# Building the routing weights of two quarters beside all up-projection units of the second quarter

## The chip, the cores and the metric

The kernel runs on one core of one Trainium2 chip. The metric is the device time of one execution in microseconds (us); less is better. The kernel before takes 2519.42 us, the median of three runs (2518.37 to 2523.47).

The core's engines each take their own instructions strictly in the order in which the program lists them, and they meet only at semaphores: PE (TensorE, matrix products), DVE (VectorE), ACT (ScalarE), POOL (GpSimd), and SP, whose queue issues most of the loads.

## The reference

One decoder layer for 256 tokens of width 2048. The first sub-layer (convolution and attention) isn't touched by the change. The second is a retrieval of single-neuron experts: 16384 experts, an expert being a pair (e1, e2) of 128 x 128, of which each token picks 16 for each of 8 heads.

```
idx = e1 * PEER_NKEYS + e2
g = jax.nn.softmax(top, axis=-1)
def chunk(args):
    xc, ic, gc = args
    u = jnp.take(w_up, ic, axis=0)
    a = jax.nn.gelu(jnp.einsum('td,tkd->tk', xc, u), approximate=False)
    return jnp.einsum('tk,tkd->td', gc * a, jnp.take(w_down, ic, axis=0))
```

Inputs and outputs are float32.

## The kernel before

The kernel computes the retrieval densely. For each of the 128 rows e1 it forms the activation gelu(x . w_up) of 128 experts (e2) for all 256 tokens, multiplies it by a routing weight that is zero where the token didn't pick the expert, and multiplies the product by w_down. Rows go in four quarters q of EQ = 32 rows. Two buffers CB[0] and CB[1], each of 128 x (32 rows x 256 tokens), hold the weighted activations of an even and an odd quarter.

**Units and halves.** Work comes as units of one 1 MB load and two halves each. `Stream.run` (line 214) writes out the order by hand: for half s it first emits "a" of half s+3, then "b" of half s+2, then whatever came due (what was appended to `after` of half s-1, in that order), then the matmuls of half s. All engines' instructions are listed in that order.

- An up half (`up_unit`, line 1233) of n = 0 or 1: "a" transposes half of a weight row on DVE (L1250, tile `wt`, 2 buffers) and casts it on ACT to the high part `hi` (L84, 4 buffers). "b" subtracts, `lo` = `wt` - `hi` (L88, 3 buffers), on POOL or on DVE, as the argument `pool_lo` says. Its 24 matmuls (L1265 to L1267) are three products of high and low parts. After every second row `up_done` (line 1285) takes two rows from PSUM through gelu on ACT.
- A down half (`down_unit`, line 1392): ACT casts weights and activations to high parts (`hi` L84, `cch` L1413), DVE subtracts both low parts (L88, `ccl` L1418), PE does 12 matmuls of 512 columns (L1435 to L1438). A quarter's down work goes in two passes, d = 0 and 1, one for each half of the output columns.
- A gate step (`gate_c`, line 1318; called by `gate_step`, line 1372) makes the routing weights of a pair of quarters for a block of NT = 8 tokens. `build` makes one-hot tiles on DVE: `oh2` (L1331), `oh1` (L1334), and three `ohg` (L1338), all bf16 from SBUF. `product` multiplies them on PE (L1347, 24 matmuls) into PSUM tile `gps`. `apply` multiplies CB[0] by the weights of the even quarter on DVE (L1354), and puts the weights of the odd quarter into CB[1] by an ACT copy (L1359). Step b does apply(b-2), build(b), product(b-1), so 32 blocks need 34 steps.

**The order around the change.** First the 32 up units of quarter 0 run, with every `lo` on POOL, and beside them the top-k selection on DVE. Then 18 up units of quarter 1 run alone ("solo"), every `lo` on POOL, with one gate step after each half. Their activations can't go into CB[1], where the weights are being put, so gelu writes them to a side tile `H` of 16 rows (L1298), and DVE multiplies them into CB[1] later (`weigh`, L1304). Then the remaining 14 up units of quarter 1, every `lo` on DVE, are interleaved with the 16 down units of quarter 0, d = 0; then come the 16 down units of d = 1; and so on. The second pair of quarters has its gate steps in quarter 1's d = 1 pass. Between units of the four interleaved parts `add_units(..., 0.25)` puts one unit of the modulation weights (L344 to L347: a 1 MB load, four ACT operations, POOL additions) after every fourth unit, 16 in all, until the list is empty.

Of the kernel before, what the change touches and what calls it, by code (L numbers as in the profile page):

```python
# [8 lines left out]
F32 = mybir.dt.float32  # L9
# [4 lines left out]
AF = mybir.ActivationFunctionType  # L14
OP = mybir.AluOpType
# [3 lines left out]
P = 128  # L19
T = 256  # L20
# [13 lines left out]
EQ = 32  # L34
# [32 lines left out]
def layer_kernel(ctx, tc, x, c, norm1_g, norm2_g, w_ada, b_ada, w_in, conv_dw, conv_db, conv_ln_g,  # L67
                 conv_ln_b, w_conv_out, b_conv_out, q_norm_g, k_norm_g, w_attn_o, w_out, peer_w_q,
                 peer_sub_keys, peer_w_up, peer_w_down, out):
    nc = tc.nc  # L70
# [6 lines left out]
    main = ctx.enter_context(tc.tile_pool(name="main", bufs=1))  # L77
# [4 lines left out]
    def split_a(h, src):  # L82
        h.hi = main.tile([P, 1024], F32R, name="hi", tag="hi", bufs=HI_BUFS)
        nc.scalar.copy(h.hi, src)  # L84
# [154 lines left out]
    st = Stream()  # L239
    T2 = {}  # L240
# [26 lines left out]
    big16 = main.tile([P, 2, D], F32, name="xin", tag="big16")  # L267
# [455 lines left out]
    def add_units(us, ada_rate=0.0):  # L723
        for u in us:
            st.add(u)
            ada_turn[0] += ada_rate
            while ada_turn[0] >= 1.0 and ada_list:
                ada_turn[0] -= 1.0
                st.add(ada_list.pop())
# [500 lines left out]
    C = {}  # L1230
    CB = []
# [42 lines left out]

    NT = 8
    late = []

    def c_row(q, r, n=1):  # L1280
        if q < 3:
            return CB[q % 2][:, r * T:(r + n) * T]
        return CB[1].rearrange("p (b e t) -> p e b t", e=EQ, t=NT)[:, r:r + n]

    def up_done(q, r, ps):

        if q % 2 == 0:
            nc.scalar.activation(c_row(q, r, 2), ps.rearrange("p r t -> p (r t)"), AF.Gelu)
            return
        if q == 1:  # L1290
            if r == 0:
                C["H"] = main.tile([P, 16, T], F32, name="H", tag="big16")
            h = C["H"][:, r % 16:r % 16 + 2].rearrange("p r t -> p (r t)")

            weigh(r - 14)
        else:
            h = T2["pool"].tile([P, 768], F32, name="hrow", tag="ohg", bufs=2)[:, 0:512]
        nc.scalar.activation(h, ps.rearrange("p r t -> p (r t)"), AF.Gelu)  # L1298
        if q == 3:
            h = h.rearrange("p (r b t) -> p r b t", r=2, t=NT)  # L1300

        def times():
            c = c_row(q, r, 2)
            nc.vector.tensor_tensor(c, c, h, op=OP.mult)  # L1304
        late.append((r, times))
        if q == 3:
            st.at(1, lambda: weigh(r + 2))

    def weigh(upto):
        while late and late[0][0] < upto:  # L1310
            late.pop(0)[1]()

    def weigh_some():
        while late:
            weigh(late[0][0] + 2)
            yield 0.6, 0

# [1 line left out]
    def gate_c(p):  # L1321
        nb = T // NT
        state = {}

        def build(b):

            pairs = lambda v: v.rearrange("p (b t) -> p b t", t=2)
            ts = slice(b * NT, (b + 1) * NT)
            nb2, ne = NT // 2, 2 * EQ
            o2 = T2["pool"].tile([P, nb2, P, 2], BF, name="oh2", tag="oh2", bufs=2)  # L1330
            nc.vector.tensor_tensor(o2, T2["iota"][:, None].to_broadcast([P, nb2, P, 2]),  # L1331
                                    pairs(T2["e2T"][:, ts])[:, :, None].to_broadcast([P, nb2, P, 2]), op=OP.is_equal)
            o1 = T2["pool"].tile([P, nb2, ne, 2], BF, name="oh1", tag="oh1", bufs=1)
            nc.vector.tensor_tensor(o1, T2["iota"][:, None, p * ne:(p + 1) * ne].to_broadcast([P, nb2, ne, 2]),  # L1334
                                    pairs(T2["e1T"][:, ts])[:, :, None].to_broadcast([P, nb2, ne, 2]), op=OP.is_equal)
            og = T2["pool"].tile([P, 3, nb2, ne, 2], BF, name="ohg", tag="ohg", bufs=2)
            for i in range(3):
                nc.vector.tensor_tensor(og[:, i], o1, pairs(T2["gp"][:, i, ts])[:, :, None].to_broadcast([P, nb2, ne, 2]),  # L1338
                                        op=OP.mult)
            state["o", b] = o2, og  # L1340

        def product(b):
            o2, og = state.pop(("o", b))
            ps = T2["ps"].tile([P, NT, 2 * EQ], F32, name="gps", tag="m", bufs=2)
            for t in range(NT):
                for i in range(3):
                    nc.tensor.matmul(ps[:, t, :], lhsT=o2[:, t // 2, :, t % 2], rhs=og[:, i, t // 2, :, t % 2],  # L1347
                                     start=i == 0, stop=i == 2)
            state["p", b] = ps.rearrange("p t e -> p e t")

        def apply(b):
            ps = state.pop(("p", b))
            cv = CB[0].rearrange("p (e t) -> p e t", e=EQ)[:, :, b * NT:(b + 1) * NT]
            nc.vector.tensor_tensor(cv, ps[:, 0:EQ], cv, op=OP.mult)  # L1354
            if p == 0:
                cv = CB[1].rearrange("p (e t) -> p e t", e=EQ)[:, :, b * NT:(b + 1) * NT]
            else:
                cv = CB[1][:, b * T:(b + 1) * T].rearrange("p (e t) -> p e t", e=EQ)
            nc.scalar.copy(cv, ps[:, EQ:2 * EQ])  # L1359

        for b in range(nb + 2):
            if 0 <= b - 2 < nb:
                apply(b - 2)
            if b < nb:
                build(b)
            if 0 <= b - 1 < nb:
                product(b - 1)
            yield
# [3 lines left out]
    def gate_step(p):  # L1372
        next(gates[p], None)

    def finish_gate(p):
        for _ in gates[p]:
            pass
# [9 lines left out]
    def down_unit(q, d, r, whole=False):  # L1387


        u = Unit(None, [])  # L1390
# [8 lines left out]
        for n in range(2):  # L1399
            rr = r + n  # L1400
            h = Half(mm=None)

            def a(h, rr=rr, n=n):
                if rr == 0 and d == 0:
                    if q % 2 == 0:
                        finish_gate(q // 2)
                    else:
                        weigh(EQ)
                split_a(h, u.raw[:, n * 1024:(n + 1) * 1024])

# [58 lines left out]

    def y_done(q, d, ps, t, c):  # L1470
        if q == 0 and d == 0 and t == 0 and c == 0:
            weigh(EQ)
            Y["acc"] = main.tile([P, 2, D], F32, name="y", tag="big16")
        cs = slice(d * 1024 + c * 512, d * 1024 + (c + 1) * 512)
        y = Y["acc"][:, t, cs]
        if q == 0 and c == 0:
            nc.scalar.copy(y, ps[t][c])
        elif q == 0:
            nc.vector.tensor_copy(y, ps[t][c])
        elif q < 3:  # L1480
            nc.vector.tensor_tensor(y, ps[t][c], y, op=OP.add)
        else:
            fin = T2["pool"].tile([P, 1024], F32, name="fin", tag="wt", bufs=2)[:, 0:512]
            nc.vector.tensor_tensor(fin, ps[t][c], Y["g2"][:, cs], op=OP.mult)
            nc.vector.tensor_tensor(fin, fin, y, op=OP.add)
            nc.sync.dma_start(out[0, t * P:(t + 1) * P, cs], fin)
# [26 lines left out]
    busy = lambda r, n: True  # L1513
    none = lambda r, n: False
    some = lambda r, n: n == 1 and r % 2 == 1
    add_units([up_unit(0, r, busy) for r in range(EQ)])
    mark_up1 = len(st.halves)
    nsolo = 18
    solo = [up_unit(1, r, busy) for r in range(nsolo)]
    for u in solo:  # L1520
        for h in u.halves:
            h.after.append(lambda: gate_step(0))
    solo[-1].halves[-1].after.append(lambda: st.spread(weigh_some()))
    add_units(solo)
    marks = []
    first_down = (0.5, 0, 1, 0)
    ada_turn[0] = 0.0
    ada_list[:] = [u for ch in range(4) for u in ada_rest(5 * D + ch * 512, gate_done(1, ch), late=True)][::-1]
    for q in range(4):
        if q < 3:  # L1530
            ups = [up_unit(q + 1, r, some if q == 2 else none) for r in range(nsolo if q == 0 else 0, EQ)]
        else:
            ups = []
        downs = [down_unit(q, 0, r) for r in range(0, EQ, 2)]
        nu, nd = len(ups), len(downs)
        seq = sorted([((i + 0.5) / nu, 0, i) for i in range(nu)] + [((i + first_down[q]) / nd, 1, i) for i in range(nd)])
        for _, kind, i in seq:
            add_units([downs[i] if kind else ups[i]], 0.25)
        assert q < 1 or not ada_list
        m1 = len(st.halves)  # L1540
        downs = [down_unit(q, 1, r, q == 1 and r % 4 == 2) for r in range(0, EQ, 2)]
        if q == 1:
            for u in downs:
                for h in u.halves:
                    h.after.append(lambda: gate_step(1))
            for h in st.halves[-2:]:
                h.after.append(lambda: gate_step(1))
        add_units(downs)
        marks.append((m1, len(st.halves)))
# [66 lines left out]
```

## Time and profile before

| | us |
|---|---|
| median of three runs | 2519.42 |
| the profiled execution | 2518.21 |
| its span, first to last instruction | 2516.4 |
| PE busy in it | 2426.6 (96%) |
| DVE busy | 1854.2 (74%) |
| ACT busy | 1120.8 (45%) |
| POOL busy | 530.3 (21%) |

The profile is of one execution. A busy PE counts matmuls that overlap each other, so its share is an upper mark; where PE has gaps, they are real. DVE's durations contain any time in which an instruction had started and could not proceed. The times of a stretch are counted from the span's start.

### The profile page before, as it was taken

The page shows a single profiled execution, that of the slowest core. Times are in us where ns is not written, and L with a number is a line of the kernel's source. Part 1 is how long each engine was busy: PE and PEld are TensorE (multiplying, and loading weights), DVE is VectorE, ACT ScalarE, POOL GpSimd, SP SyncE. Part 2 cuts the span into 40 slices and gives each one's busy share as a digit, 9 for nine tenths or more (in the row PEclk, how much of TensorE's full clock was granted, in tenths as well). Part 3 has the DMA queues.
Part 4 walks back from the last instruction along what each step waited for, and adds up shares of the span by engine and source line. Part 5 has one row for each costly group of instructions (what it writes and reads, how often), then busy time and mean ns, then how long its engine had stood idle before and what let it go on. Part 6 is the DMA issues. An engine that isn't in the chain of part 4 may idle for free.

```text
span 2516.4 us, 39750 instructions
## 1 busy us (share of the span) xinstructions
PE 2426.6 (96%) x15728; PEld 2056.6 (82%) x15728; DVE 1854.2 (74%) x2642; ACT 1120.8 (45%) x1477; POOL 530.3 (21%) x262
## 2 busy tenths in 40 slices
PE   7999889999999899988999999999999999999998
PEld 4667677777766799988889988999987899988877
DVE  2655679886454569897998787877799777667776
ACT  5333345444334444443335555555443344445454
POOL 1000000000000007786552234332000111124023
PEclk9999999999999999999999999999999999999999
DMA  9887346777899978777557866899844777766563
GB/s 329 297 301 251 117 136 210 257 251 267 279 298 294 204 159 178 158 167 152 110 124 220 234 218 194 222 226 238 204 156 135 185 181 185 188 186 214 194 209 117
DMA packets 261178, 518.73 MB, mean 206 GB/s; under 512 B 16400, under 2 KB 57568, under 8 KB 260352
## 3 DMA queue, kind: packets, MB, share of 16 engines
q1 hardware_dynamic: 258912, 507.61, 70.4%
q0 software_dynamic: 2048, 8.58, 1.0%
q8 instruction: 123, 2.02, 0.4%
q14 instruction: 63, 0.52, 0.1%
q10 hardware_dynamic: 32, 0.01, 0.0%
HBM read 511.94 MB, written 4.19 MB: 205 GB/s over the span
## 4 chain that ended last, share of the span: by engine, by line
PE 71%; DVE 10%; POOL 3%; issue 2%; DMA 1%; ACT 1%; SPq 0%; DVEq 0%; POOLq 0%; ACTq 0%
PE aps L1267 6%; PE aps L1265 6%; PE aps L1266 6%; PE y L1435 6%; PE y L1436 6%; PE y L1438 5%; PE z L429 5%; PE z L431 4%; PE z L430 4%; PE z L1436 3%; PE z L1438 3%; PE z L1435 3%; POOL lo L88 3%; DVE wt L1250 2%; PE ada L330 2%
## 5 line engine op out<-in xcount | busy, mean ns | idle before, releaser
L88 DVE TENSOR_TENSOR lo<-raw,hi 128x1024 fp32r<-128x1024 f32 x456 | 561.8, 1237 | 376.3 <-issue 112.6
L84 ACT CAST hi<-raw 128x1024 fp32r<-128x1024 f32 x504 | 526.6, 1051 | 520.6 <-PE zv L559 103.1
L1267 PE MATMUL aps<-h2hi,lo 128*128 128x256 f32 x2048 | 582.0, 284 | 8.6 <-POOL lo L88 8.5
L1265 PE MATMUL aps<-h2hi,hi 128*128 128x256 f32 x2048 | 584.3, 285 | 0.4 <-ACT hi L84 0.4
L1266 PE MATMUL aps<-h2lo,hi 128*128 128x256 f32 x2048 | 580.7, 284 | 0.0
L84 ACT CAST hi<-wt 128x1024 fp32r<-128x1024 f32 x256 | 269.3, 1052 | 470.7 <-DVE wt L1250 427.6
L88 POOL TENSOR_TENSOR lo<-wt,hi 128x1024 fp32r<-128x1024 f32 x116 | 292.7, 2529 | 611.1 <-PE aps L1267 497.1
L1267 PEld LDWEIGHTS aps<-h2hi,lo 128*128 128x128 f32 x2048 | 394.0, 192 | 11.2 <-POOL lo L88 11.2
L1265 PEld LDWEIGHTS aps<-h2hi,hi 128*128 128x128 f32 x2048 | 394.1, 192 | 2.6 <-ACT hi L84 0.6
L1266 PEld LDWEIGHTS aps<-h2lo,hi 128*128 128x128 f32 x2048 | 394.3, 193 | 2.0 <-issue 0.2
L1250 DVE STREAM_TRANSPOSE wt<-raw 128x1024 f32<-128x1024 f32 x256 | 315.8, 1237 | 28.2 <-POOL lo L88 23.7
L1418 DVE TENSOR_TENSOR ccl<-C,cch 128x256 fp32r<-128x256 f32 x248 | 198.9, 803 | 96.7 <-PE z L1438 57.6
L1435 PE MATMUL y<-hi,cch 128*128 128x512 f32 x608 | 241.1, 397 | 0.0
L1436 PE MATMUL y<-lo,cch 128*128 128x512 f32 x608 | 237.3, 390 | 0.0
L88 DVE TENSOR_TENSOR lo<-wt,hi 128x1024 fp32r<-128x1024 f32 x140 | 171.8, 1229 | 27.3 <-PE aps L1267 14.0
L1438 PE MATMUL y<-hi,ccl 128*128 128x512 f32 x608 | 187.6, 390 | 0.0
L88 POOL TENSOR_TENSOR lo<-raw,hi 128x1024 fp32r<-128x1024 f32 x48 | 117.0, 2436 | 245.9 <-PE z L1436 123.6
L347 POOL TENSOR_TENSOR acc<-acc,raw 128x512 f32<-128x512 f32 x60 | 101.4, 1689 | 261.0 <-ACT raw L346 240.3
L1413 ACT CAST cch<-C 128x256 fp32r<-128x256 f32 x248 | 99.8, 403 | 123.6 <-PE z L1436 101.9
L1436 PE MATMUL z<-lo,cch 128*128 128x512 f32 x384 | 149.5, 389 | 2.2 <-DVE lo L88 2.2
L1435 PE MATMUL z<-hi,cch 128*128 128x512 f32 x384 | 149.5, 389 | 1.0 <-ACT cch L1413 1.0
L1438 PEld LDWEIGHTS y<-hi,ccl 128*128 128x128 f32 x608 | 114.2, 188 | 24.4
(295 smaller groups left out, 3965.7 us busy)
## 6 DMA issues: line engine op xcount, KB each, us to landing
raw<-in_peer_w_up_dram SPq DMA_DIRECT2D x512, 256.0 KB, 6.0
raw<-in_peer_w_down_dram SPq DMA_DIRECT2D x128, 1024.0 KB, 5.1
raw<-in_w_ada_dram SPq DMA_DIRECT2D x86, 1024.0 KB, 7.1
raw<-in_w_in_dram SPq DMA_DIRECT2D x73, 1024.0 KB, 5.3
raw<-in_w_out_dram SPq DMA_DIRECT2D x64, 256.0 KB, 5.2
raw<-in_peer_w_q_dram SPq DMA_DIRECT2D x64, 256.0 KB, 7.1
raw<-in_w_in_dram SPq DMA_DIRECT2D x22, 512.0 KB, 8.9
raw<-in_w_ada_dram SPq DMA_DIRECT2D x20, 512.0 KB, 5.2
```

Source lines behind the costliest of these rows:

```text
L84: nc.scalar.copy(h.hi, src)
L88: eng.tensor_tensor(h.lo, src, h.hi.bitcast(F32), op=OP.subtract)
L347: nc.gpsimd.tensor_tensor(acc, acc, src, op=OP.add)
L429: nc.tensor.matmul(z, lhsT=ah, rhs=hi[:, kk], start=first, stop=False)
L1250: nc.vector.transpose(wt.rearrange("p j g a -> p g j a"), u.raw.rearrange("p (g j a) -> p g j a", g=4, a=32)[:, :, n * 8:(n + 1) * 8, :])
L1265: nc.tensor.matmul(z, lhsT=hi[:, jj], rhs=qh["hi"][:, j, :], start=j == 0, stop=False)
L1266: nc.tensor.matmul(z, lhsT=hi[:, jj], rhs=qh["lo"][:, j, :], start=False, stop=False)
L1267: nc.tensor.matmul(z, lhsT=lo[:, jj], rhs=qh["hi"][:, j, :], start=False, stop=j == NK - 1)
L1418: nc.vector.tensor_tensor(cl, row, ch, op=OP.subtract)
L1435: nc.tensor.matmul(z, lhsT=ch, rhs=hi, start=first, stop=False)
L1436: nc.tensor.matmul(z, lhsT=ch, rhs=lo, start=False, stop=False)
L1438: nc.tensor.matmul(z, lhsT=cl, rhs=hi, start=False, stop=last)
```

## The change

All 32 up units of quarter 1 run alone before any down unit; each unit's first half has its `lo` on DVE, the second on POOL. The 34 gate steps are spread over the first 62 of these 64 halves. Rows and blocks of tokens now meet in either order. `have["t"]` counts the tokens whose weights are in CB[1], `have["rows"]` the rows whose activations are there. When two rows are finished, `up_done` puts gelu straight into CB[1] for tokens without weights, and for those with weights into `H`, which DVE multiplies into CB[1] at once. When a block of weights is finished, `apply` multiplies by it the rows that are there (a second DVE operation from PSUM), and copies it for the other rows. The deferred `weigh` of quarter 1 and `weigh_some` go. Quarter 0's d = 0 part then has down units only.

```diff
@@ up_done
         if q == 1:
-            if r == 0:
-                C["H"] = main.tile([P, 16, T], F32, name="H", tag="big16")
-            h = C["H"][:, r % 16:r % 16 + 2].rearrange("p r t -> p (r t)")
-            weigh(r - 14)
-        else:
-            h = T2["pool"].tile([P, 768], F32, name="hrow", tag="ohg", bufs=2)[:, 0:512]
+            c = c_row(q, r, 2).rearrange("p (r t) -> p r t", r=2)
+            t0 = have["t"]
+            if t0 < T:
+                nc.scalar.activation(c[:, :, t0:], ps[:, :, t0:], AF.Gelu)
+            if t0 > 0:
+                if "H" not in C:
+                    C["H"] = main.tile([P, 16, T], F32, name="H", tag="big16")
+                h = C["H"][:, r % 16:r % 16 + 2, 0:t0]
+                nc.scalar.activation(h, ps[:, :, 0:t0], AF.Gelu)
+                nc.vector.tensor_tensor(c[:, :, 0:t0], c[:, :, 0:t0], h, op=OP.mult)
+            have["rows"] = r + 2
+            return
...
@@ gate_c, apply
-            if p == 0:
-                cv = CB[1].rearrange("p (e t) -> p e t", e=EQ)[:, :, b * NT:(b + 1) * NT]
-            else:
+            if p == 1:
                 cv = CB[1][:, b * T:(b + 1) * T].rearrange("p (e t) -> p e t", e=EQ)
-            nc.scalar.copy(cv, ps[:, EQ:2 * EQ])
+                nc.scalar.copy(cv, ps[:, EQ:2 * EQ])
+                return
+            cv = CB[1].rearrange("p (e t) -> p e t", e=EQ)[:, :, b * NT:(b + 1) * NT]
+            r = have["rows"]
+            if r:
+                nc.vector.tensor_tensor(cv[:, :r], ps[:, EQ:EQ + r], cv[:, :r], op=OP.mult)
+            if r < EQ:
+                nc.scalar.copy(cv[:, r:], ps[:, EQ + r:2 * EQ])
+            have["t"] = (b + 1) * NT
...
+    half = lambda r, n: n == 1
-    nsolo = 18
-    solo = [up_unit(1, r, busy) for r in range(nsolo)]
-    for u in solo:
-        for h in u.halves:
+    solo = [up_unit(1, r, half) for r in range(EQ)]
+    steps = T // NT + 2
+    for i, h in enumerate(h for u in solo for h in u.halves):
+        if i < 2 * EQ - 2 and (i + 1) * steps // (2 * EQ - 2) > i * steps // (2 * EQ - 2):
             h.after.append(lambda: gate_step(0))
-    solo[-1].halves[-1].after.append(lambda: st.spread(weigh_some()))
...
-        if q < 3:
-            ups = [up_unit(q + 1, r, some if q == 2 else none) for r in range(nsolo if q == 0 else 0, EQ)]
-        else:
-            ups = []
+        ups = [up_unit(q + 1, r, some if q == 2 else none) for r in range(EQ)] if q in (1, 2) else []
```

## Rows read from the trace of the kernel before

**Rows 1.** Busy time by stretch: PE, PEld, DVE, ACT, POOL; clock, DMA share, GB/s.
```profile
1157.40:1318.50 161.10, 142.52 (x1635) 135.46 (x1634) 154.05 (x232) 52.58 (x80) 88.19 (x35) 0.97 0.52 118
1318.50:1487.40 168.90, 168.90 (x1066) 153.54 (x1065) 133.64 (x131) 92.87 (x128) 44.39 (x28) 1.00 0.80 231
1487.40:1575.00 87.60, 86.59 (x382) 71.38 (x381) 66.26 (x56) 46.85 (x66) 37.28 (x15) 1.00 0.60 191
1575.00:1850.00 275.00, 275.00 (x1948) 259.48 (x1947) 217.15 (x203) 140.28 (x181) 59.50 (x34) 1.00 0.87 219
```

**Rows 2.** Waits in 1155:1320: total us, times, longest.
```profile
ACT hi L84 <- DVE wt L1250: 101.6, 35, 5.7
POOL lo L88 <- PE aps L1267: 65.5, 31, 7.5
```

**Rows 3.** Timeline, steady solo half: start us, us, engine, line, operation [idle before].
```profile
1248.78 2.58 POOL L88 TENSOR_TENSOR lo<-wt,hi 128x1024 fp32r<-128x1024 f32 x1 [1.70 <-PE aps L1267]
1249.01 1.24 DVE L1250 STREAM_TRANSPOSE wt<-raw 128x1024 f32<-128x1024 f32 x1
1250.17 0.39 DVE L1354 TENSOR_TENSOR C<-gps,C 128x256 f32<-128x256 f32 x1
1250.48 1.42 DVE L1331 TENSOR_TENSOR oh<-iota_rep,e2T 128x1024 bf16<-128x1024 bf16 x1
1252.28 1.09 DVE L1338 TENSOR_TENSOR ohg<-oh,gp 128x512 bf16<-128x512 bf16 x3
1253.29 1.24 DVE L1250 STREAM_TRANSPOSE wt<-raw 128x1024 f32<-128x1024 f32 x1
1257.35 2.57 POOL L88 TENSOR_TENSOR lo<-wt,hi 128x1024 fp32r<-128x1024 f32 x1 [1.72 <-PE aps L1267]
```

**Rows 4.** The same view, early solo halves.
```profile
1188.43 2.41 POOL L88 TENSOR_TENSOR lo<-wt,hi 128x1024 fp32r<-128x1024 f32 x1 [4.26 <-PE aps L1267]
1189.36 2.02 DVE L1331 TENSOR_TENSOR oh<-iota_rep,e2T 128x1024 bf16<-128x1024 bf16 x1
1191.75 3.24 DVE L1338 TENSOR_TENSOR ohg<-oh,gp 128x512 bf16<-128x512 bf16 x3
```

**Rows 5.** The same view, down pass d = 1 of quarter 0.
```profile
1504.92 2.41 POOL L88 TENSOR_TENSOR lo<-raw,hi 128x1024 fp32r<-128x1024 f32 x1 [2.41 <-PE z L1436]
1505.34 2.27 DVE L1418 TENSOR_TENSOR ccl<-C,cch 128x256 fp32r<-128x256 f32 x1 [0.74 <-PE z L1438]
```

**Rows 6.** The same view, a gate step of the second pair, POOL idle.
```profile
1903.29 1.22 DVE L88 TENSOR_TENSOR lo<-raw,hi 128x1024 fp32r<-128x1024 f32 x1
1904.42 0.42 DVE L1418 TENSOR_TENSOR ccl<-C,cch 128x256 fp32r<-128x256 f32 x1
1904.76 0.42 DVE L1354 TENSOR_TENSOR C<-gps,C 128x256 f32<-128x256 f32 x1
1905.09 0.68 DVE L1331 TENSOR_TENSOR oh<-iota_rep,e2T 128x1024 bf16<-128x1024 bf16 x1
1907.15 1.22 DVE L88 TENSOR_TENSOR lo<-raw,hi 128x1024 fp32r<-128x1024 f32 x1
```

**Rows 7.** The same view, first matmuls of a product, two up halves, two down halves.
```profile
1173.89 0.89 PE L1347 MATMUL gps<-ohg,oh 128*128 128x64 bf16 x24
1174.62 0.36 PE L1265 MATMUL aps<-h2hi,hi 128*128 128x256 f32 x1
1315.59 0.28 PE L1265 MATMUL aps<-h2hi,hi 128*128 128x256 f32 x1
1318.47 0.40 PE L1435 MATMUL y<-hi,cch 128*128 128x512 f32 x1
1323.94 0.28 PE L1265 MATMUL aps<-h2hi,hi 128*128 128x256 f32 x1
```

**Rows 8.** Groups in 1155:1320 by form: busy us, mean ns, idle before.
```profile
L84 ACT CAST hi<-wt 128x1024 fp32r<-128x1024 f32 x37 | 38.9, 1050 | 107.8 <-DVE wt L1250 101.6 <-PE aps L1266 6.2
L1298 ACT ACTIVATE H<-aps 128x512 f32<-128x512 f32 x8 | 4.7, 591 | 0.0
```

More of the change, by code (lines that the diff above doesn't have):

```diff
@@ L1278, in layer_kernel @@
     late = []
+    have = {"rows": 0, "t": 0}
     def c_row(q, r, n=1):
@@ L1290, in up_done @@
         if q == 1:
-            if r == 0:
-                C["H"] = main.tile([P, 16, T], F32, name="H", tag="big16")
-            h = C["H"][:, r % 16:r % 16 + 2].rearrange("p r t -> p (r t)")
-            weigh(r - 14)
-        else:
-            h = T2["pool"].tile([P, 768], F32, name="hrow", tag="ohg", bufs=2)[:, 0:512]
+            c = c_row(q, r, 2).rearrange("p (r t) -> p r t", r=2)
[10 more added lines that the diff above has]
+            return
+        h = T2["pool"].tile([P, 768], F32, name="hrow", tag="ohg", bufs=2)[:, 0:512]
         nc.scalar.activation(h, ps.rearrange("p r t -> p (r t)"), AF.Gelu)
-        if q == 3:
-            h = h.rearrange("p (r b t) -> p r b t", r=2, t=NT)
+        h = h.rearrange("p (r b t) -> p r b t", r=2, t=NT)
         def times():
@@ L1305, in up_done @@
         late.append((r, times))
-        if q == 3:
-            st.at(1, lambda: weigh(r + 2))
+        st.at(1, lambda: weigh(r + 2))
     def weigh(upto):
@@ L1311, in weigh @@
             late.pop(0)[1]()
[L1313 to L1316, printed above, removed]
     def gate_c(p):
@@ L1406, in a @@
                         finish_gate(q // 2)
-                    else:
+                    elif q == 3:
                         weigh(EQ)
@@ L1471, in y_done @@
         if q == 0 and d == 0 and t == 0 and c == 0:
-            weigh(EQ)
             Y["acc"] = main.tile([P, 2, D], F32, name="y", tag="big16")
@@ L1529, in layer_kernel @@
     for q in range(4):
-        if q < 3:
-            ups = [up_unit(q + 1, r, some if q == 2 else none) for r in range(nsolo if q == 0 else 0, EQ)]
-        else:
-            ups = []
+        ups = [up_unit(q + 1, r, some if q == 2 else none) for r in range(EQ)] if q in (1, 2) else []
         downs = [down_unit(q, 0, r) for r in range(0, EQ, 2)]
```

## The prediction

> **What bounds the kernel now.** I read the page's totals first, then a table of stretches, then the waits and the timeline of the one stretch in which PE isn't full. PE is busy 96% of the span, so only its gaps can be won, and the table shows where they are [rows 1]: the solo stretch, 1157.4 to 1318.5, has PE at 142.5 of 161.1 us and DVE at 154.1. The interleaved stretch behind it, the d = 1 pass and the next quarter have PE full or within 1 us of it. The two stretches that the change rebuilds end at 1487.4, 330.0 us after they began.
>
> In the solo stretch the waits name DVE [rows 2]: ACT waits 101.6 us for transposes, and POOL 65.5 us for PE to free a `lo` buffer. The timeline says why DVE is full [rows 3]. A steady half takes 4.28 us from one transpose to the next. The one-hot operation L1331 has 1.42 us in it, though it takes 0.68 with POOL idle [rows 6]: it starts at 1250.48, POOL's subtraction ends at 1251.36, and DVE's operation 0.54 later. In the early halves the same thing costs more [rows 4]: L1331 2.02 us, and the three `ohg` 3.24 instead of 1.09, each with a POOL operation inside it. It isn't a matter of bf16: the float32 `ccl` takes 2.27 us instead of 0.42 beside POOL's 2.41 [rows 5, 6]. So **a DVE operation with both inputs in SBUF stands still while POOL's subtraction runs**; the transpose (one input) and L1354 (one input in PSUM) do not [rows 3].
>
> **What the change takes, adds and moves.** The same matmuls run, so PE needs what it needed. An up half with its product takes 1174.62 - 1173.89 = 0.73 for the product and 2.88 (1318.47 - 1315.59) for the rest; two down halves take 5.47 [rows 7]. New solo stage: 64 x 2.88 + 32 x 0.73 = 208 us of PE; the 32 down halves alone 87.5, as in the d = 1 pass, 87.6 [rows 1]. Together 295.5 against 330.0: **34.5 us is all that can be won.**
>
> DVE's work with POOL silent [rows 3, 6]: 64 transposes x 1.16 = 74.2 (1250.17 - 1249.01); 32 `lo` x 1.13 = 36.2; 32 times `apply` 0.33 and the five one-hot operations 2.06 (1907.15 - 1905.09) = 76.5. The second `apply` on rows already there costs between 0 and 0.33 as rows fill up, taken as 0.2: 6.4. The weighing in `up_done` grows with the tokens from 0 to 512 elements, half a `lo`, so 0 to 0.6, taken as 0.3: 16 x 0.3 = 5. Sum 198 us. That is below PE's 208; what decides is how much of POOL's 32 x 2.45 = 78 us falls on DVE operations that can't run beside it.
>
> I walk through it with the order of the program and these prices. Time 0 is the end of the last `ohg` of a gate step; a step comes every second half, and PE waits for it.
>
> *Step in a half whose `lo` is DVE's (even s).* PE: product and matmuls, then POOL may begin the `lo` of half s+3. In the steady solo half that was 1257.35 - 1253.37 = 3.98 after the `ohg` [rows 3]; POOL ends at 6.4. DVE meanwhile does two transposes, `lo`, both `apply`: 1.16 + 1.16 + 1.13 + 0.53 = 3.98, and then wants L1331, just as POOL has begun. It waits to 6.4 and takes 2.06: **8.5 us** for two halves, and PE needs 6.5. Every fourth half brings `up_done`: H is ready when the cast behind the second transpose (2.32 + 1.05) and two gelu parts (between 0.59, the price of the whole [rows 8], and 1.18; taken 0.7) are done, 4.1, and the weighing waits for POOL too: 6.4 + 0.3 + 0.53 + 2.06 = 9.3, or, if it slips in ahead of POOL, 8.9. I take 9.1.
>
> *Step in a half whose `lo` is POOL's (odd s).* POOL begins behind the cast of its own half: 1.16 + 1.08 = 2.3, and ends at 4.75. DVE does transpose, `lo`, transpose, both `apply` to 4.0, waits to 4.75, takes 2.06: **6.8**. With `up_done`, H is ready at 3.0, behind POOL's start, so DVE stands from 2.3 to 4.75, then 0.3 + 1.16 + 0.53 + 2.06: **8.8**. This is the wait that the change adds; queued behind it on DVE are the next transpose and the whole gate step, and through them ACT's cast and PE's product.
>
> *Sum.* The 34 steps fall on halves 2 to 10, 22 to 30, 42 to 52 (even) and 11 to 21, 31 to 41, 53 to 61 (odd), and 62. Up to the last build (half 59): 13 even gaps, 7 with weighing, 7 x 9.1 + 6 x 8.5 = 115; 13 odd, 7 x 8.8 + 6 x 6.8 = 102; five junctions with one half between steps, three even to odd at 3.75 (transpose, `apply`, 2.06) and two odd to even at 7.4 (POOL falls among the one-hots) = 26. Start to the first built block: three halves and a blocked step, 12. Behind the last build: a product and three halves, 9.4. Together 264 us, then 87.5 of down halves: 352 against 330, **+22 us.** Ties between POOL and DVE and the short first weighings take off an estimated 2: +20.
>
> Edits at no cost. The interleaved stretch gave 1 us to waits (168.9 against 28 x 2.88 + 87.5 = 168.1), which goes. Down halves alone need of DVE 1.22 + 0.42 and of ACT 1.05 + 0.4 in 2.73 us, covered by PE. ACT's split gelu and copies lie in a stage where ACT is a third busy [rows 1]. SP issues the same loads; the solo units now want 1 MB per some 8 us, less than the interleaved stretch did. Three of the 16 modulation units move from quarter 0's part into the next [rows 1], the last row, where DVE has 58 us free of 275 and DMA 13%; three units bring some 20 us of POOL additions. Covered; were it not, it costs at most those 20.
>
> The Trainium skill, "Perfetto Trace Analysis", section "Optimization Strategy", advises to interleave stretches that have different most-contended engines. It speaks against this change, which takes up halves (hungry for DVE) away from down halves (not). The trace agrees: the interleaved stretch has PE full with DVE at 79% [rows 1].
>
> **Rivals.**
> *PE binds.* POOL's 78 us fall beside the 74 us of transposes and the `apply`. DVE then needs 198 plus little, PE's 208 rules: 208 + some 8 at the ends + 87.5 = 303.5, -26 us: 2492. It decides where a POOL `lo` costs DVE below (208 - 198) / 32 = 0.3 us. For it: half as many POOL operations per half as before. Against: before, with a transpose in every half, one cost 1.2 (DVE's 161.1 less 36 x 1.16 + 32 x 2.39 = 118, over 36), and none of the patterns above gets below 0.7. The same page of the Trainium skill, section "Identifying the Most-Contended Engine", takes the engine of highest occupancy as the limit; by it this rival holds.
> *A draw.* Each POOL `lo` costs what it did, 1.2: 198 + 38 + some 6 at the ends = 242, +87.5 = 329.5: 2518.
> *Weighing in front.* Where H came before POOL began, the 14 weighing gaps would cost some 1.2 less: +4, 2522, the low end of the forecast.
> *Everything collides.* All 78 us fall on DVE: 198 + 78 + 9 = 285, +42: 2560, with PE's clock possibly lower in its gaps (0.97 in the solo stretch now [rows 1]).
>
> **How the numbers follow.** The profiled execution took 2518.2 us, 1.8 more than its span and 1.2 less than the median. 2518.2 + 20 = 2538. Chances: forecast, weighing in front included, 0.73; draw 0.13; PE binds 0.09; all collides 0.05. A measurement tells 0.2% (5 us) from no change. Slower by more: 0.75 (forecast and collision, less the lowest part of the forecast); within: 0.12; faster: 0.13 (PE binds, and the draw's lower side). The range goes from the draw's lower half, 2514, to halfway between forecast and collision, 2550.
>
> **What would show it.** Right: the solo stage about 264 us long (its end near 1421), PE at 78 to 82% there, DVE at 97% or more; periods of 8.5 to 9.3 us in the even runs, 6.8 to 8.8 in the odd; L1331 near 2.4 us longer than 0.68 in the even runs; weighings of 2 us and more in the odd runs; the down halves at 2.73 with PE full, ending near 1508. Wrong: PE above 90% in the solo stage with L1331 at 0.68 (PE binds), or PE waiting in the down halves or behind 1575.

## The result, and the profile after

The changed kernel takes 2545.93 us (median of four runs, 2545.77 to 2547.07). The kernel before, on the same chip beside it, took 2518.89 (2518.21 to 2523.47). The ratio is 1.0102, with a 95% interval of 1.0089 to 1.0115. The change costs 27 us; the forecast was 20.

Line numbers moved with the change: the one-hot operations L1331, L1334 and L1338 are now L1333, L1336 and L1340; the product L1347 is L1349; `apply` L1354 is L1356, and its second operation, on rows already there, is L1364; the weighing of two finished rows is L1303. A down half's first matmul, L1435, is L1443.

The table of stretches of the changed kernel (window, length, then busy time and number of instructions of PE, PEld, DVE, ACT, POOL; granted clock, DMA share, GB/s) is to be read beside [rows 1]. The first row is the new solo stage, the second the down units of quarter 0, d = 0, the third the d = 1 pass, the fourth the next interleaved part:

```profile
1155.90:1422.80 266.90, 232.06 (x2306) 224.65 (x2305) 247.21 (x333) 83.18 (x128) 78.15 (x32) 0.94 0.56 127
1422.80:1510.70 87.90, 87.90 (x395) 72.95 (x393) 68.07 (x67) 55.70 (x87) 28.57 (x16) 1.00 0.69 233
1510.70:1598.30 87.60, 87.60 (x387) 72.38 (x387) 63.13 (x55) 46.15 (x64) 36.62 (x16) 1.00 0.64 199
1598.30:1873.00 274.70, 273.70 (x1938) 258.15 (x1937) 219.73 (x204) 148.55 (x196) 78.81 (x45) 1.00 0.89 229
```

Two stretches of 161.1 and 168.9 us have become two of 266.9 and 87.9. The down halves run with PE full, as in the d = 1 pass. PE's idle time lies in the solo stage, and there DVE is the busiest.

The waits of that stage (engine, tile and line, what was waited for: us in total, times, longest) name the same two engines as [rows 2], and new ones below them:

```profile
ACT hi L84 <- DVE wt L1250: 149.2, 47, 5.5
POOL lo L88 <- PE aps L1267: 93.6, 12, 12.6
POOL lo L88 <- ACT hi L84: 62.1, 14, 6.7
PE gps L1349 <- DVE ohg L1340: 29.9, 16, 5.0
...
DVE C L1303 <- ACT H L1302: 7.4, 14, 0.9
DVE wt L1250 <- POOL lo L88: 6.5, 4, 2.2
```

POOL is let go in two ways: by PE in the even runs (gate steps in halves whose `lo` is DVE's), by the cast of its own half in the odd ones. (In four even gaps the view names ACT's `H`, which ended at that moment; POOL began as long after the `ohg` there as where it names PE.) These are the two cases that the prediction walked through. The product L1349 waits for `ohg`, the last of the one-hot operations. The weighing L1303 waits little for `H`; its cost lies in its duration.

The timeline (start, duration, engine, line, operation, idle time before it and what ended it) shows an even run, first a gap without weighing, then one with it:

```profile
1265.79 2.95 POOL L88 TENSOR_TENSOR lo<-wt,hi 128x1024 fp32r<-128x1024 f32 x1 [5.38 <-PE aps L1267]
1265.80 0.68 DVE L1333 TENSOR_TENSOR oh<-iota_rep,e2T 128x1024 bf16<-128x1024 bf16 x1
1266.40 2.62 DVE L1336 TENSOR_TENSOR oh<-iota_rep,e1T 128x512 bf16<-128x512 bf16 x1
1269.06 1.09 DVE L1340 TENSOR_TENSOR ohg<-oh,gp 128x512 bf16<-128x512 bf16 x3
...
1270.07 2.36 DVE L1250 STREAM_TRANSPOSE wt<-raw 128x1024 f32<-128x1024 f32 x2
1272.50 1.23 DVE L88 TENSOR_TENSOR lo<-wt,hi 128x1024 fp32r<-128x1024 f32 x1
1274.13 2.40 POOL L88 TENSOR_TENSOR lo<-wt,hi 128x1024 fp32r<-128x1024 f32 x1 [5.40 <-ACT H L1302]
1274.16 2.59 DVE L1303 TENSOR_TENSOR C<-C,H 128x192 f32<-128x192 f32 x1 [0.43 <-ACT H L1302]
1278.23 1.10 DVE L1340 TENSOR_TENSOR ohg<-oh,gp 128x512 bf16<-128x512 bf16 x3
```

In the first gap POOL begins as L1333 does. L1333 keeps its 0.68, and POOL's subtraction takes 2.95 us instead of 2.41: the DVE operation that got in first holds POOL up. The operation behind it, L1336, takes 2.62 us instead of 0.41. In the second, the `ohg` before it ends at 1270.15, POOL begins 3.98 later, and the weighing of 192 elements, 0.36 alone, lasts until POOL is done: 2.59. The next `ohg` ends 9.18 after the one before.

And an odd run, in the same view, a gap without weighing and one with it:

```profile
1302.58 2.42 POOL L88 TENSOR_TENSOR lo<-wt,hi 128x1024 fp32r<-128x1024 f32 x1 [4.38 <-ACT hi L84]
1304.18 1.37 DVE L1333 TENSOR_TENSOR oh<-iota_rep,e2T 128x1024 bf16<-128x1024 bf16 x1
1305.92 1.10 DVE L1340 TENSOR_TENSOR ohg<-oh,gp 128x512 bf16<-128x512 bf16 x3
...
1309.39 2.40 POOL L88 TENSOR_TENSOR lo<-wt,hi 128x1024 fp32r<-128x1024 f32 x1 [4.38 <-ACT hi L84]
1309.90 2.19 DVE L1303 TENSOR_TENSOR C<-C,H 128x272 f32<-128x272 f32 x1 [0.62 <-ACT H L1302]
```

Here transposes and `apply` cover the first POOL operation but for 0.7 us in L1333; the second stops the weighing until POOL is done: 2.19 us, where a weighing of 272 elements takes 0.43 alone (shown below).

**Where the 27 us are.** The span went from 2516.4 to 2544.0. Up to the last gelu of quarter 0 (1159.00 before, 1157.36 after) the profiled execution was 1.6 ahead. From there to the end of the down halves it took 353.3 us against 328.4: +24.9. From there to the end of the third product of the second pair's gate steps (1862.77 and 1888.89) 378.2 against 375.4: +2.8. Then nothing for some 569 us, and +1.5 behind that, where the granted clock was 0.50 from 2458.1 to 2461.4 (before, 1.00 at that place). The rebuilt stretch is the loss.

### The profile page after: what moved, and what is told of

It reads as the page before. It is cut to its first block, busy times and chain, and to the rows that moved or that the text cites. A ratio compares the mean times of both kernels' runs of the same rounds, so it can differ in the third digit from the quotient of the medians.

```text
span 2544.0 us, 39834 instructions
## 1 busy us (share of the span) xinstructions
PE 2442.0 (96%) x15728; PEld 2070.9 (81%) x15728; DVE 1881.8 (74%) x2677; ACT 1121.0 (44%) x1491; POOL 520.3 (20%) x258
## 3 DMA queue, kind: packets, MB, share of 16 engines
q0 software_dynamic: 2048, 8.58, 1.0%
## 4 chain that ended last, share of the span: by engine, by line
PE 69%; DVE 11%; ACT 2%; POOL 2%; issue 2%; DMA 2%; SPq 0%; DVEq 0%; ACTq 0%; POOLq 0%
PE y L1443 6%; PE aps L1265 6%; PE aps L1267 6%; PE aps L1266 5%; PE y L1444 5%; PE y L1446 5%; PE z L429 5%; PE z L431 5%; PE z L430 5%; PE z L1444 3%; PE z L1446 3%; PE z L1443 3%; DVE wt L1250 3%; POOL lo L88 2%; PE ada L330 2%
## 5 line engine op out<-in xcount | busy, mean ns | idle before, releaser
L88 POOL TENSOR_TENSOR lo<-wt,hi 128x1024 fp32r<-128x1024 f32 x112 | 280.1, 2505 | 656.1 <-PE aps L1267 448.3
L1443 PE MATMUL y<-hi,cch 128*128 128x512 f32 x608 | 242.2, 398 | 0.0
L1443 PE MATMUL z<-hi,cch 128*128 128x512 f32 x384 | 150.3, 391 | 0.0
```

The source lines that it names most:

```text
L88: eng.tensor_tensor(h.lo, src, h.hi.bitcast(F32), op=OP.subtract)
L1443: nc.tensor.matmul(z, lhsT=ch, rhs=hi, start=first, stop=False)
```

## The experiments

The theory: DVE stands still in operations with two SBUF inputs while POOL subtracts, so the time is set by what DVE wants at the moment when POOL begins, and not by how much work either has. Its rivals: the amount of DVE's work; PE as the bound; the moved modulation units; the way in which rows and blocks are now joined (the extra `apply` and weighing).

**POOL silent.** All 64 subtractions of the solo units go to DVE.

```diff
-    solo = [up_unit(1, r, half) for r in range(EQ)]
+    solo = [up_unit(1, r, none) for r in range(EQ)]
```

> The kernel after, with every `lo` of the solo stage on DVE: 32 subtractions (36 us) move from POOL to DVE, and POOL has nothing to do in the stage. Port theory (a POOL subtraction stops DVE's operations with two SBUF inputs): DVE needs 198 + 36 = 235 us and nothing stops it, so the solo stage falls from 267 to about 245 us and the time from 2546 to about 2524; one-hot operations L1333 at 0.68 us throughout. Rival, the amount of DVE's work sets the stage: it grows by about 36 us, to 2580.

Measured: 2522.41 us, ratio to the kernel before 1.0005 (0.9995 to 1.0015). DVE got some 38 us more work (32 x 1.19), and the kernel became 24 us faster. The solo stage ends at 1404.0 instead of 1422.8. The groups of DVE there (busy us, mean ns, idle before):

```profile
L88 DVE TENSOR_TENSOR lo<-wt,hi 128x1024 fp32r<-128x1024 f32 x63 | 74.8, 1187 | 2.0 <-PE aps L1267 2.0
...
L1333 DVE TENSOR_TENSOR oh<-iota_rep,e2T 128x1024 bf16<-128x1024 bf16 x32 | 21.7, 678 | 0.0
```

All 32 L1333 take 0.68. Most gaps without weighing are 7.1 to 7.3 (all 6.7 to 7.8) instead of 7.9 to 8.5 (even) and 6.8 (odd): beside the odd steps POOL's help was worth 0.4 us a gap, beside the even ones it cost over 1. On the mean one POOL subtraction of the changed kernel costs DVE an estimated (18.8 + 38) / 32 = 1.8 us, where doing it itself costs 1.19. Spreading the gate steps over all rows, with its extra `apply`, weighing, and moved modulation units, costs nothing measurable in sum against the kernel before; the POOL halves cost the 24.

**Where the gate steps stand.** Two kernels with the same instructions in another order: gate steps only in halves whose `lo` is POOL's (odd), or only in those whose `lo` is DVE's (even). Two steps double up at the start, and the last two, which build nothing, are emitted with "a" of the first down half.

```diff
-        if i < 2 * EQ - 2 and (i + 1) * steps // (2 * EQ - 2) > i * steps // (2 * EQ - 2):
+        for _ in range((i % 2 == 0 and i < 60) + (i in (0, 2))):        # odd
+        for _ in range((i % 2 == 1 and i < 60) + (i in (1, 3))):        # even
             h.after.append(lambda: gate_step(0))
```

> The kernel after, with the same 34 gate steps all in halves whose `lo` is POOL's (two steps in the first two of these). Theory of the two patterns: 28 gaps at a mean of 7.8 us, stage about 244 us, time about 2525. Rival, POOL and DVE meet at random and only the sums count: within 4 us of 2546.

> The kernel after, with the same 34 gate steps all in halves whose `lo` is DVE's. Theory of the two patterns: 28 gaps at a mean of 8.75 us, stage about 270 us, time about 2550, some 25 us more than with the steps in the other halves. Rival, POOL and DVE meet at random and only the sums count: no difference between the two, both within 4 us of 2546.

Measured: odd 2531.86 us, 1.0047 (1.0031 to 1.0064); even 2566.58, 1.0181 (1.0164 to 1.0198). The solo stages end at 1408.6 and 1448.3. They are 35 us apart, where the amount of work is the same and would give no difference. Gaps are 6.8 without and 8.5 to 9.1 with weighing (odd), 8.3 to 8.5 and 8.9 to 9.6 (even, a pair of 6.2 and 11.3 aside), much the same as in the odd and even runs of the changed kernel. Both came out slower than expected, odd by 7 us and even by 17: the doubled steps took two gaps of 10.4 (odd), of 11.5 and 13.0 (even), and even gaps with weighing were a little longer than allowed for. In the timelines the weighing stands behind POOL's operation in both, first odd, then even:

```profile
1260.51 2.41 POOL L88 TENSOR_TENSOR lo<-wt,hi 128x1024 fp32r<-128x1024 f32 x1 [4.39 <-ACT hi L84]
1261.02 2.11 DVE L1303 TENSOR_TENSOR C<-C,H 128x192 f32<-128x192 f32 x1 [0.62 <-ACT H L1302]
1265.73 1.09 DVE L1340 TENSOR_TENSOR ohg<-oh,gp 128x512 bf16<-128x512 bf16 x3
```

```profile
1255.05 2.40 POOL L88 TENSOR_TENSOR lo<-wt,hi 128x1024 fp32r<-128x1024 f32 x1 [4.25 <-ACT H L1302]
1255.08 2.54 DVE L1303 TENSOR_TENSOR C<-C,H 128x144 f32<-128x144 f32 x1 [0.44 <-ACT H L1302]
```

**The weighing a half later.** In the changed kernel, the weighing is emitted one half later, when POOL is done and `H` has long been ready.

```diff
-                nc.vector.tensor_tensor(c[:, :, 0:t0], c[:, :, 0:t0], h, op=OP.mult)
+                st.at(1, lambda: nc.vector.tensor_tensor(c[:, :, 0:t0], c[:, :, 0:t0], h, op=OP.mult))
```

> The kernel after, with the multiplication in `up_done` emitted one half later, behind the gate step, where POOL's subtraction is over. Theory that this multiplication is an added wait on the path (it stops at POOL's operation and the next transpose is queued behind it): the odd gaps with weighing go from 8.8 to 7.1 us (7 of them), the even ones from 9.1 to 8.8 (7): -14 us, 2532. Rival, it stands where DVE would wait anyway for POOL or PE: within 3 us of 2546.

Measured: 2530.56 us, 1.0038 (1.0024 to 1.0053): 15 us less than the changed kernel, 12 of them in the solo stage (end at 1410.7). But for the first gap of a run, odd gaps with weighing went from 8.5 to 9.1 down to 6.8 to 7.1, the ones behind them from 6.8 to between 6.9 and 7.3; even gaps went from 8.9 to 9.5 with weighing to 8.2 to 8.4. A weighing of 272 elements is short again:

```profile
1310.45 0.43 DVE L1303 TENSOR_TENSOR C<-C,H 128x272 f32<-128x272 f32 x1
```

**Both together.** Gate steps in POOL's halves, weighing a half later.

> odd and late together: gate steps in POOL's halves, weighing behind the gate step. odd had periods of 6.8 us and 8.7 with weighing; the theory of the two patterns gives 7.1 instead of 8.7 for 14 of them: 2532 - 22 = 2510, ahead of the kernel before by some 0.4%. Rival, the two gains are the same one: 2531.

Measured: 2506.3 us (five runs, 2505.51 to 2510.92), ratio to the kernel before 0.9951 (0.9937 to 0.9965): 0.5% faster than the kernel before, and by the two ratios 1.5% faster than the changed kernel, with the same arithmetic. Two steps of its timeline, and its solo stage in the view of stretches:

```profile
1257.55 1.09 DVE L1340 TENSOR_TENSOR ohg<-oh,gp 128x512 bf16<-128x512 bf16 x3
1258.57 0.35 DVE L1303 TENSOR_TENSOR C<-C,H 128x192 f32<-128x192 f32 x1
...
1261.29 2.42 POOL L88 TENSOR_TENSOR lo<-wt,hi 128x1024 fp32r<-128x1024 f32 x1 [4.65 <-ACT hi L84]
...
1264.63 1.10 DVE L1340 TENSOR_TENSOR ohg<-oh,gp 128x512 bf16<-128x512 bf16 x3
```

```profile
1156.60:1387.30 230.70, 219.38 (x2304) 214.03 (x2303) 222.15 (x334) 83.25 (x130) 76.83 (x32) 0.98 0.64 146
```

The weighing of the same 192 elements takes 0.35 instead of 2.11, POOL's subtraction lies beside a transpose and `apply`, and a gap is 7.08 with the weighing in it. POOL does as much here as in the changed kernel (76.8 us against 78.2), with 36 us less.

**POOL silent in the kernel before.** The 18 solo units of the kernel before with every `lo` on DVE (`busy` becomes `none` in `solo`).

> The kernel before, with every `lo` of its 18 solo units on DVE instead of POOL: 36 x 1.13 = 41 us more work for DVE in a stretch where DVE was busy 154 of 161 us. Port theory: DVE needs 36 x 2.29 + 77 = 160 us and nothing stops it: 161 as before, within 4 us of 2519. Rival, amount of work: 2519 + 35 to 41.

Measured: 2519.98 us, 1.0001 (0.9991 to 1.001), with the down halves ending at 1487.8 (before: 1487.4). POOL's 36 subtractions won nothing there either: 1.2 us of standing, as the prediction worked out, for 1.19 of work. This is what the draw rested on; it was the price of the old pattern and didn't carry over.

**Which POOL operation stops DVE.** Two kernels with POOL silent, as above, and one extra idle POOL operation a unit, in the place of its subtraction: one subtracts two constant tiles, the other sets a tile of 128 x 2048 to zero. ACT reads one column of what it wrote, so that it keeps its place, and `H` gives 8 of its 16 rows to the idle tile (lines shortened).

```diff
+                if q == 1 and n == 1:                     # in "a"
...
+                    nc.scalar.copy(C["seen"], C["idle"][:, 0:1])
+                if q == 1 and n == 1:                     # in "b", reads:
+                    nc.gpsimd.tensor_tensor(C["idle"][:, 0:1024], <h2hi, first half>, <h2hi, second half>, op=OP.subtract)
+                                                           # or, writes:
+                    nc.gpsimd.memset(C["idle"], 0.0)
```

> all_dve (every `lo` on DVE), plus an operation on POOL that nothing needs, once for every unit of the solo stage, behind the cast of its second half: a subtraction of two constant SBUF tiles of 128x1024 into unused rows of `H`, some 2.4 us. No result waits for it; a small ACT copy paces it. Port theory: DVE stops for it as in the kernel after, by 1.4 us in the odd gaps and 2 in the even ones and more with weighing: 2522 + some 45, 2567. Rival, what cost time in the kernel after was that results came late from POOL: 2522 to 2526.

> As pool_reads, but the idle operation on POOL is a memset of 128x2048 in `H`, which reads nothing from SBUF. If only POOL's reads stop DVE: 2522 to 2527. If any POOL operation does: 2522 plus half to the whole of the memset's length for each of the 32.

Measured (two runs each): with the subtraction 2593.68 us, 1.0292 (1.0273 to 1.0311), with the memset 2538.36, 1.0073 (1.0054 to 1.0091). Both are above what was expected, 2567 and at most 2527. The solo stage ends at 1457.7 with the one and 1403.3 with the other; with POOL silent it was 1404.0. The timelines, first of the subtraction, then of the memset:

```profile
1245.24 2.41 POOL L1265 TENSOR_TENSOR H<-h2hi 128x1024 f32<-128x1024 f32 x1 [7.36 <-ACT seen L1260]
1246.24 2.49 DVE L88 TENSOR_TENSOR lo<-wt,hi 128x1024 fp32r<-128x1024 f32 x1
```

```profile
1257.30 1.81 POOL L1265 MEMSET H<- 128x2048 f32 x1 [6.42 <-ACT seen L1260]
1257.54 0.68 DVE L1340 TENSOR_TENSOR oh<-iota_rep,e2T 128x1024 bf16<-128x1024 bf16 x1
```

(L1340 is `oh2` in that kernel.) A subtraction that nothing needs makes DVE's `lo` 2.49 instead of 1.19; a memset of 1.81 us leaves the one-hot beside it at 0.68. In the solo stage the idle subtraction costs 54 us (45 were expected), 1.7 each, the memset nothing. Nothing waits for either but the one-column copy that both kernels have, so it isn't late data. The two operations differ in kind and length; what the subtraction does and the memset doesn't is read SBUF.

The Trainium skill, "SBUF — State Buffer", section "Who interferes with whom", says that a VectorE instruction with two SBUF inputs contends with a GpSimd instruction that reads SBUF, and not with one that only writes it. The trace agrees: 54 us against none.

The memset kernel was yet 16 us slower than the one with POOL silent, all of it behind the solo stage, and the subtraction kernel lost 17 there. In both the 128x512 matmuls took 396 ns instead of 389.

**The small tile alone.** To see whether that was the idle operation or the small tile `seen`, which may shift the places of other tiles in SBUF: POOL silent, plus that tile alone, 4 bytes a partition, written once.

```diff
+                if q == 1 and n == 1 and "seen" not in C:
+                    C["seen"] = T2["pool"].tile([P, 1], F32, name="seen")
+                    nc.gpsimd.memset(C["seen"], 0.0)
```

> all_dve with one more SBUF tile of 4 bytes per partition, written once, at the place where pool_reads and pool_writes have theirs; no other work. Those two lost some 14 us behind the solo stage, where their down matmuls took 396 ns instead of 389. If the tile's shift of what lies behind it in SBUF does that: 2522 + 14 = 2536, with down matmuls at 396 ns. If what they did on POOL and ACT in the solo stage does: 2522.

Measured (two runs): 2540.74 us, 1.0083 (1.0054 to 1.0113), the solo stage ending at 1403.8. The down matmuls by group (busy us, mean ns) in this kernel and in the one with POOL silent, both at a granted clock of 1.00:

```profile
L1447 PE MATMUL y<-lo,cch 128*128 128x512 f32 x116 | 45.8, 395 | 0.0
L1446 PE MATMUL y<-hi,cch 128*128 128x512 f32 x115 | 45.6, 396 | 0.0
```

```profile
L1444 PE MATMUL y<-lo,cch 128*128 128x512 f32 x119 | 46.3, 389 | 0.0
L1443 PE MATMUL y<-hi,cch 128*128 128x512 f32 x118 | 45.9, 389 | 0.0
```

The tile alone makes the difference, and the two idle kernels must be read by their solo stages. That it does so by shifting the tiles behind it is not shown: the traces hold no addresses. In the changed kernel and in the one before these matmuls take 389, as with POOL silent, so none of the 27 us is from this.

## Why the prediction was right

**The reading of the bound** held. DVE with two SBUF inputs stands while POOL subtracts, and transposes and operations that read PSUM don't (1.25 and 0.39 us beside the subtraction at 1302.58, as in [rows 3]). The silent kernel and the idle subtraction each show the standing by itself, and the memset shows that POOL being busy is not enough.

**The walk, step by step.** From the first `ohg` to the last the changed kernel took 244.4 us; the walk gave 115 + 102 + 26 = 243.

| | walk | measured |
|---|---|---|
| start to first built block | 12 | 13.1 |
| 13 even gaps | 115 (8.5; 9.1 weighing) | 117.5 (7.9 to 8.5; 8.9 to 9.4, first of a later run 11.3 and 11.4) |
| 13 odd gaps | 102 (6.8; 8.8 weighing) | 106.1 (6.8; 8.5 to 9.1, one of 10.1 without) |
| 5 junctions | 26 (3.75; 7.4) | 20.8 (3.6 to 3.8; 4.8 to 4.9) |
| behind the last build | 9.4 | 9.4 |
| solo stage | 264 | 266.9 |
| down halves alone | 87.5 | 87.9 |

In eight of the even gaps POOL began 3.97 to 3.99 behind the `ohg`, what the walk took from the steady half before [rows 3]; in three, each behind a gap with weighing, 5.4 to 5.5. In nine of the odd gaps it began at 2.37 or 2.38 (taken 2.3), in the first of each run at 4.5 to 5.7. The terms that were off are small, and that the sum comes so near is in part luck: the gaps were 6.6 us longer than in the walk, the junctions 5.2 shorter. At the two odd to even junctions the prediction let POOL fall among the one-hots at once; it fell one gap later: 4.8 and 11.3 to 11.4, together 16.1 to 16.3, instead of 7.4 and 9.1, together 16.5. Even gaps without weighing were up to 0.3 shorter, the first 0.65; there POOL often slips in behind L1333 and stops L1336 or the first `ohg` instead. Six even gaps, not seven, had a weighing: when the first two rows were done no weights were there yet. Odd gaps with weighing grew with the tokens. And one odd gap of 6.8, the last run's first, was 10.1.

**The term that was off** is the 2 us taken off for ties and short weighings: nothing came off, and the stage was 3 longer than the sum. With the 22 of the plain sum the rebuilt stretch (+24.9) is met within 3.

**The rest of the 27** was not in the forecast: the 2.8 us around 1873 and the 1.5 at the end, less the 1.6 by which this execution was ahead. In the first, the column sums of the last modulation unit stand right behind a product that had waited, and matmuls behind them run at the lower clock level, 0.63 instead of 0.39:

```profile
1872.62 1.50 PE L1349 MATMUL gps<-ohg,oh 128*128 128x64 bf16 x24 [0.86 <-DVE ohg L1340]
1873.95 1.48 PE L359 MATMUL gateps<-ones,acc 128*128 128x1 f32 x8
...
1875.87 0.63 PE L1444 MATMUL y<-lo,cch 128*128 128x512 f32 x1
```

The granted clock there is the lower of its two levels (1.2 and 2.4 GHz), after a wait of PE of 0.86 us for an `ohg`; at the same place of the program the kernel before has 1.00 (1848 to 1855):

```profile
1874.40:1881.10 6.70, 6.70 (x28) 5.21 (x28) 6.01 (x13) 1.08 (x3) 0.00 (x0) 0.50 0.40 148
```

The wait itself goes with the moved units: POOL's additions of one of them now lie beside the first down halves of the pass, and DVE's `lo` takes 2.17 us there instead of 1.23:

```profile
1862.13 7.28 POOL L347 TENSOR_TENSOR acc<-acc,raw 128x512 f32<-128x512 f32 x4 [13.51 <-ACT raw L346]
1866.09 2.17 DVE L88 TENSOR_TENSOR lo<-raw,hi 128x1024 fp32r<-128x1024 f32 x1 [1.45 <-ACT cch L1421]
```

But the kernels with POOL silent and with both edits place the modulation units alike, have the same wait (0.89 and 0.87) and don't show the 2.8. The 1.5 at the end is another such spell; it stands in the kernel with POOL silent and in the one of before with POOL silent too, and not in the one with both edits or in before. So the moved units cost nothing measurable by themselves, as forecast; why the clock fell just there in the changed kernel stays open.

**The rivals.** PE as the bound was wrong: its need of 208 us in the solo stage is 59 below the 266.9 it took. The Trainium skill's rule for the most-contended engine ("Perfetto Trace Analysis", section "Identifying the Most-Contended Engine"), which stood behind this rival, goes by busy time (for TensorE it asks for other measures, which the prediction didn't use); the measurement decided against the rival, and the kernels with other places for the steps say why: a sum over an engine doesn't contain where it is stopped. The draw took 1.2 us for each POOL `lo`; it was 1.8. "Weighing in front" came true only in the first gaps of runs (four weighings of 0.23 to 0.51 us). Not everything collided: DVE was busy 247 us, 49 more than the 198 of its sum with POOL silent, so by this estimate 49 of POOL's 78 us fell on it; with both edits, at 222, it is 24. The section "Optimization Strategy" of the same page of the Trainium skill spoke against the change, and the sign came out its way, but not for its reason: with both edits the same un-interleaved order beats the kernel before by 0.5%.

**The marks** in the profile: stage end near 1421 (1422.8), down halves at 1508 (1510.7) with PE full, the periods, and weighings of 2 us and more in the odd runs, came as said. L1331 (now L1333) waited in one even gap only (2.85); elsewhere in the even runs its neighbours did. The two shares were off: PE 87% busy instead of 78 to 82, since at a granted clock of 0.94 the up matmuls were busy 202 us instead of the 184 of the sum, and the first matmuls of a product that waits count as busy; DVE 93% instead of 97, since the weighing waits 7.4 us for `H`, transposes 6.5 for POOL to free `wt`, and `lo` 3.7 for PE and ACT.

## What to carry to other kernels

Where one engine's operations stop another's, put neither the sum of the work nor the number of operations into the estimate first, but which operation is next on the one when the other begins; here that alone was worth 35 us between two orders of the same instructions. Handing work from the stopped engine to the one that stops it can lose: 32 subtractions of 1.19 us, given away, cost 1.8 each. Whether it loses depends on the place: with both edits a gap is 6.8 to 7.4, where with POOL silent it was mostly 7.1 to 8.5 (the order of both edits with POOL silent was not run). Before giving up a change, look for the operations that can run beside the other engine (here transposes and reads from PSUM) and move the rest by one half.

## What the runs showed of the hardware that was not expected

- A tile of 4 bytes a partition, written once, made 128x512 float32 matmuls take 396 ns instead of 389 at the same granted clock of 1.00, and the kernel 18 us slower than the one without it (2540.74 against 2522.41, each beside its own runs of the kernel before at 2519.26 and 2522.62). It may shift other tiles in SBUF; why that should matter is open.
- POOL's memset of 128x2048, 1.81 us long, cost the solo stage nothing; its subtraction of 128x1024, 2.41 us, stops a DVE operation with two SBUF inputs that comes behind it until it is done, bf16 ones of 0.41 us as well as float32 ones. A DVE operation that got in first isn't stopped; then the subtraction takes longer (2.95).
- The granted clock of the solo stage fell as the stage grew, though not in proportion: 0.98 where it took 230.7 us, 0.94 at 246.0 (POOL silent) and at 266.9, and 0.90 with the idle subtractions, at 300.3. PE's busy time for the same matmuls was 219, 226, 232 and 244 us there.
